# Squares, 1/rms and two staged reads in other places of a hybrid block's start-up order

## The chip, the core and the metric

The kernel runs on one core of a Trainium2 chip. Times are device microseconds (us) of one execution. TensorE is called PE here, VectorE DVE, ScalarE ACT, GpSimd POOL, and SyncE, which only sends DMAs here, SP. Times inside the execution count from the start of the profiled span.

## The reference

One layer: an RMSNorm of x (512 tokens, 2048 wide), one input projection whose columns are q, k, v, an attention gate, the input xr of a linear recurrence (LRU) and its gate, then attention beside the LRU, a norm and a gate on each, and an output projection added to x.

```python
def rms_norm(x, w):
    y = xf * lax.rsqrt(jnp.mean(xf * xf, axis=-1, keepdims=True) + EPS)
    return y * w
...
h = rms_norm(x, norm_w)
proj = jnp.einsum('bsd,de->bse', h, w_in)
q, k, v, g_attn, xr, g_lru = jnp.split(proj, SPLITS, axis=-1)
attn_out = attention_group(q, k, v, q_norm_w, k_norm_w)
lru_out = lru_group(xr, conv_w, conv_b, lru_wa, lru_ba, lru_wx, lru_bx, lru_lambda)
mixed = jnp.concatenate([rms_norm(attn_out, attn_norm_w) * jax.nn.silu(g_attn),
                         rms_norm(lru_out, lru_norm_w) * jax.nn.silu(g_lru)], axis=-1)
return x + jnp.einsum('bse,ed->bsd', mixed, w_out)
```

All in float32.

## The kernel before

**Products.** Every float32 operand is split into a high part and the rest, and a product is three matmuls (`mm3`, lines 153 to 155). A tile of x is `x` in the profile's rows, a tile of weights is read as `wr`, its high part cast on ACT to `wh` (line 228) and its rest made on DVE as `wl` (line 229).

**The norm.** The gain `norm_w` is multiplied into x's tiles. The factor 1/rms of a token isn't: the projection runs on the x without it, and the factor is multiplied in when a result leaves PSUM. It needs the squares of all of x, so it is known late: `xsquare` (line 276) sums the squares of a chunk on ACT (line 278; for the first two chunks on DVE), `xstats` adds the chunks' sums on DVE (line 402), takes the power -0.5 on POOL (`rsqrt_mean`, lines 374 and 375), and `rows` lays the result out on DVE (lines 386 to 389), spreads it over all partitions with one matmul by ones (line 396) and copies that to `rbc` (line 397).

**The start.** x comes in eight chunks of 256 columns (`L`, 512 KB each). The first two are turned by PE. Each of the others is turned in blocks on DVE (`B`, line 291), written aside to DRAM in four DMAs (`D`, line 306), read back in whole rows in one DMA (`R`, line 313), multiplied by the gain on ACT (line 361) and split on ACT and DVE (`V`, lines 367 and 368). The read waits until the write has landed. Beside this the chunk's weights are read (`W`, line 215) and split (`S`, lines 228 and 229), and its squares taken (`Q`). PE multiplies chunk after chunk for the first half of xr (`proj_feat`, accumulators `pj`), and after chunk 1 puts two chunks of the second half (accumulators `mm`) in between.

**What sets the order.** SP and POOL, and for the start ACT and DVE too, run in the order in which the program issues; each engine runs its own list in order, and a waiting instruction holds up all behind it. The table `moves` (lines 1245 to 1256) gives that order: a key `(c, e)` is the place behind PE's step e of chunk c, a letter an action and the digit its chunk (`Z` takes the next step of `xstats`: the first one the sum and the power, the second one the layout). After key `(6, 0)` ACT and DVE go back to the scheduler, which orders what follows by its own estimates.

**After the start.** Two steps of chunk 7 later PE runs the spreading matmul, finishes chunk 7, takes 36 matmuls of the second half, and then the first product of the LRU (`lru_pair`). Its input is the accumulator times `rbc` (`ev`, lines 1286 and 503), put through a convolution (one step on ACT, line 536, three on DVE, line 541), and split (lines 546 and 547, `k`). The LRU's own weights are read by SP (line 515).

Of the kernel before, what the change touches and what calls it, by code (L numbers as in the profile page):

```python
# [63 lines left out]
def hybrid_kernel(  # L64
# [814 lines left out]
    P1, Q6, Q5, Q7, P2, Q3, Q4 = 0, 5, 4, 3, 2, 6, 1  # L879
# [356 lines left out]
    def vectors(_):  # L1236
# [19 lines left out]
    }  # L1256

    def move(step):
# [244 lines left out]
```

## Time and profile before

| what | value |
|---|---|
| time, 3 runs | 630.44 us median (629.39 to 632.7) |
| the profiled execution's own time | 633.15 us |
| its span | 631.4 us |
| mean granted PE clock | 0.995 |
| DMA, mean over the span | 207 GB/s |

The span is what lies between the first and the last recorded instruction. A row of the timeline gives the start, the duration and the operation, `out<-in`, and in brackets how long the engine had been idle and what released it. A matmul's duration overlaps the next one's, so PE's pace is read from the distance of two starts.

### The profile page before, as it was taken

The page shows a single profiled execution, that of the slowest core. Times are in us where ns is not written, and L with a number is a line of the kernel's source. Part 1 is how long each engine was busy: PE and PEld are TensorE (multiplying, and loading weights), DVE is VectorE, ACT ScalarE, POOL GpSimd, SP SyncE. Part 2 cuts the span into 40 slices and gives each one's busy share as a digit, 9 for nine tenths or more (in the row PEclk, how much of TensorE's full clock was granted, in tenths as well). Part 3 has the DMA queues.
Part 4 walks back from the last instruction along what each step waited for, and adds up shares of the span by engine and source line. Part 5 has one row for each costly group of instructions (what it writes and reads, how often), then busy time and mean ns, then how long its engine had stood idle before and what let it go on. Part 6 is the DMA issues. An engine that isn't in the chain of part 4 may idle for free.

```text
span 631.4 us, 8289 instructions
## 1 busy us (share of the span) xinstructions
PE 622.8 (99%) x2732; PEld 511.8 (81%) x2732; DVE 495.5 (78%) x789; ACT 360.8 (57%) x648; POOL 106.0 (17%) x142
## 2 busy tenths in 40 slices
PE   9999899999999999999999999999999999999997
PEld 7877688888888888888888888888888888888886
DVE  6674877997979896787887788549989867787776
ACT  4478379988966741645575557339355544433441
POOL 3000211111103352512123222100210001010010
PEclk9999899999999999999999999999999999999999
DMA  8998857584976479589669647842995777797262
GB/s 280 315 306 295 241 108 187 152 191 132 224 237 209 125 162 273 134 191 271 189 188 269 198 136 200 250 117 67 241 282 178 229 238 234 283 335 243 71 200 100
DMA packets 76219, 130.76 MB, mean 207 GB/s; under 512 B 6953, under 2 KB 31121, under 8 KB 76177
## 3 DMA queue, kind: packets, MB, share of 16 engines
q1 hardware_dynamic: 68064, 112.75, 57.5%
q0 software_dynamic: 7936, 17.36, 14.2%
q8 instruction: 21, 0.34, 0.2%
q10 hardware_dynamic: 176, 0.14, 0.1%
q14 instruction: 22, 0.17, 0.1%
HBM read 111.87 MB, written 39.32 MB: 239 GB/s over the span
## 4 chain that ended last, share of the span: by engine, by line
PE 83%; DVE 7%; DMA 6%; ACT 2%; issue 1%; SPq 1%; POOL 0%; ACTq 0%; DVEq 0%
PE pj L154 16%; PE pj L155 15%; PE pj L153 15%; PE mm L1066 14%; PE pj L1066 11%; PE mm L154 4%; PE mm L153 4%; PE mm L155 4%; DMA wr<-in_w_in_dram 2%; DMA xu<-xd 2%; DVE wl L229 1%; DMA xd<-xu 1%; DVE k L541 1%; DVE xu L291 1%; DVE b L585 1%
## 5 line engine op out<-in xcount | busy, mean ns | idle before, releaser
L228 ACT CAST wh<-wr 128x512 fp32r<-128x512 f32 x142 | 84.3, 617 | 83.3 <-PE pj L154 33.1
L155 PE MATMUL pj<-x,wl 128*128 128x512 f32 x304 | 119.1, 392 | 0.2 <-DVE wl L229 0.2
L154 PE MATMUL pj<-x,wh 128*128 128x512 f32 x304 | 118.7, 391 | 0.0
L153 PE MATMUL pj<-x,wh 128*128 128x512 f32 x304 | 118.7, 390 | 0.0
L229 DVE TENSOR_TENSOR wl<-wr,wh 128x512 fp32r<-128x512 f32 x144 | 98.8, 713 | 23.8 <-ACT wh L228 21.3
L914 ACT CAST wh<-wr 128x1024 fp32r<-128x1024 f32 (+1 forms) x72 | 60.7, 860 | 75.7 <-PE mm L1066 37.2
L915 DVE TENSOR_TENSOR wl<-wr,wh 128x1024 fp32r<-128x1024 f32 (+1 forms) x72 | 68.7, 983 | 29.0 <-ACT wh L914 28.9
L153 PE MATMUL pj<-wh,x 128*128 128x512 f32 x192 | 74.9, 390 | 0.0
L154 PE MATMUL pj<-wl,x 128*128 128x512 f32 x192 | 74.8, 390 | 0.0
L155 PE MATMUL pj<-wh,x 128*128 128x512 f32 x192 | 74.7, 389 | 0.0
L155 PEld LDWEIGHTS pj<-x,wl 128*128 128x128 f32 x304 | 57.3, 188 | 13.3 <-DVE wl L229 1.3
L153 PEld LDWEIGHTS pj<-x,wh 128*128 128x128 f32 x304 | 57.2, 188 | 11.9 <-ACT wh L228 0.3
L154 PEld LDWEIGHTS pj<-x,wh 128*128 128x128 f32 x304 | 57.2, 188 | 11.9
L938 POOL DMA_DIRECT2D t<-in_w_out_dram x40 | 33.3, 890 | 141.8 <-DMA t<-in_w_out_dram 84.1
L1066 PE MATMUL mm<-wh,ml 128*128 128x512 f32 x126 | 49.0, 389 | 0.0
L1066 PE MATMUL mm<-wh,mh 128*128 128x512 f32 x126 | 49.0, 389 | 0.0
L1066 PE MATMUL mm<-wl,mh 128*128 128x512 f32 x126 | 49.0, 389 | 0.0
L153 PEld LDWEIGHTS pj<-wh,x 128*128 128x128 f32 x192 | 36.0, 188 | 8.1 <-ACT ev L628 0.5
L154 PEld LDWEIGHTS pj<-wl,x 128*128 128x128 f32 x192 | 36.1, 188 | 7.8 <-DVE wl L229 0.5
L155 PEld LDWEIGHTS pj<-wh,x 128*128 128x128 f32 x192 | 36.0, 188 | 7.5
L738 POOL TENSOR_SCALAR p<-p,sm 128x512 f32<-128x512 f32 x32 | 24.2, 759 | 89.6 <-DVE sm L737 89.6
L1066 PE MATMUL pj<-wl,mh 128*128 128x512 f32 (+1 forms) x100 | 38.5, 385 | 0.0
(229 smaller groups left out, 1176.2 us busy)
## 6 DMA issues: line engine op xcount, KB each, us to landing
wr<-in_w_in_dram SPq DMA_DIRECT2D x71, 512.0 KB, 5.0
wr<-in_w_out_dram SPq DMA_DIRECT2D x21, 512.0 KB, 5.6
t<-in_w_out_dram POOLq DMA_DIRECT2D x40, 256.0 KB, 7.6
wr<-t SPq DMA_DIRECT2D x40, 256.0 KB, 5.4
pd<-u SPq DMA_DIRECT2D x16, 512.0 KB, 3.0
pt<-pd SPq DMA_DIRECT2D x64, 128.0 KB, 3.7
t<-in_w_out_dram SPq DMA_DIRECT2D x24, 256.0 KB, 4.8
wr<-in_w_out_dram SPq DMA_DIRECT2D x22, 256.0 KB, 5.0
```

What stands on the lines that cost most here:

```text
L153: nc.tensor.matmul(acc, lh, rh, start=start, stop=False)
L154: nc.tensor.matmul(acc, lh, rl, start=False, stop=False)
L155: nc.tensor.matmul(acc, ll, rh, start=False, stop=stop)
L228: copy(hi, raw[:, k, :]).ins,
L229: nc.vector.tensor_sub(lo, raw[:, k, :], f(hi)).ins,
L291: nc.vector.transpose(u[:, :, :, t, :].rearrange("p b k r -> p k b r"), src.rearrange("p (k b c) -> p k b c", k=2, c=B),)
L541: nc.vector.scalar_tensor_tensor(xc[:, d0:d1], xr[:, d0 + o : d1 + o], v1(R_CW + j * NB + n), xc[:, d0:d1], op0=ALU.mult, op1=ALU.add,)
L738: last_pool[0] = nc.gpsimd.tensor_scalar(p, p, sm, 0.0, op0=ALU.mult, op1=ALU.add).ins
L914: nc.scalar.copy(hi[:, to], b)
L915: nc.vector.tensor_sub(lo[:, to], b, f(hi[:, to]))
L938: nc.gpsimd.dma_start(dst, src, accum_op=ALU.add)
L1066: nc.tensor.matmul(dst[s][:, es], lh[:, ts_], rh[:, es], start=i == ends_[0] and j == 0, stop=i == ends_[1] and j == 2,)
```

## The change

Only the table is edited. With letters as above:

```diff
-        (1, 0, 1): "V2 S2 W3 R4 L6 Q1 B5 D5",
-        (2, 0): "V3 S3 W4 L7 B6 D6 R5 W5",
-        (3, 0): "V4 Q2 S4 B7 D7 R6 W6",
-        (4, 0): "C2 V5 S5 Q5 W7 R7",
-        (5, 0): "C3 V6 S6 Q6",
-        (6, 0): "V7 S7 Q7 Q4 Z0 Z0 C3",
+        (1, 0, 1): "V2 S2 Q2 W3 R4 L6 Q1 B5 D5",
+        (2, 0): "V3 S3 W4 L7 B6 R5 D6 W5",
+        (3, 0): "V4 Q4 S4 Q5 B7 R6 D7 W6",
+        (4, 0): "C2 V5 S5 Q6 W7 R7",
+        (5, 0): "C3 V6 S6 Q7 Z0",
+        (6, 0): "V7 S7 Z0 C3",
```

Nothing is added or taken away: the rounds of squares of chunks 2, 4, 5, 6 and 7 stand in other places, the sum and power stand ahead of chunk 7's work, and the reads of chunks 5 and 6 stand ahead of the writes of chunks 6 and 7.

On ACT, from chunk 6's weights on, before (`wh_643` and `wh_647` are chunk 6's weights, `xu_526` is chunk 7's x read back, and the two rows `b_..,ssq` ahead of `wh_823` are the squares of chunks 7 and 4):

```order
L228 CAST wh_643<-wr_537 128x512
L228 CAST wh_647<-wr_537 128x512
L278 ACTIVATE b_69_402,ssq<-b_69_402 128x256 x4
L361 ACTIVATE xu_526<-xu_526,nw 128x4x128 x2
L367 CAST x_116_681<-xu_526 128x4x4x32
L367 CAST x_118_685<-xu_526 128x4x4x32
L228 CAST wh_689<-wr_600 128x512
L228 CAST wh_693<-wr_600 128x512
L278 ACTIVATE b_82_463,ssq<-b_82_463 128x256 x4
L278 ACTIVATE b_36_257,ssq<-b_36_257 128x256 x4
L228 CAST wh_823<-wr_821 128x512
```

and in the changed kernel (`wh_651` and `wh_655` are chunk 6's weights, `b_82_467` is chunk 7):

```order
L228 CAST wh_651<-wr_545 128x512
L228 CAST wh_655<-wr_545 128x512
L278 ACTIVATE b_82_467,ssq<-b_82_467 128x256 x4
L361 ACTIVATE xu_534<-xu_534,nw 128x4x128 x2
L367 CAST x_116_693<-xu_534 128x4x4x32
L367 CAST x_118_697<-xu_534 128x4x4x32
L228 CAST wh_701<-wr_608 128x512
L228 CAST wh_705<-wr_608 128x512
L228 CAST wh_823<-wr_821 128x512
```

Chunk 7's squares are now where chunk 6's were, and none stand behind chunk 7's weights.

On DVE at the same place, before (`xsum` is the sum, `x_117` and `x_119` are chunk 7's x, `wl_690` and `wl_694` its weights, `two` and `k_124` the layout, `lc` small constants of the LRU):

```order
L368 TENSOR_TENSOR x_117_682<-xu_526,x_116_681 128x4x4x32
L368 TENSOR_TENSOR x_119_686<-xu_526,x_118_685 128x4x4x32
L229 TENSOR_TENSOR wl_690<-wr_600,wh_689 128x512
L229 TENSOR_TENSOR wl_694<-wr_600,wh_693 128x512
L402 TENSOR_REDUCE xsum<-ssq 128x4
L386 CAST two<-rstd 64x4
```

and in the changed kernel, on to the copy of 1/rms (`rbc`); the layout's rows `two` and `k_124` read as before and are left out between the two pieces:

```order
L402 TENSOR_REDUCE xsum<-ssq 128x4
L368 TENSOR_TENSOR x_117_694<-xu_534,x_116_693 128x4x4x32
L368 TENSOR_TENSOR x_119_698<-xu_534,x_118_697 128x4x4x32
L229 TENSOR_TENSOR wl_702<-wr_608,wh_701 128x512
L229 TENSOR_TENSOR wl_706<-wr_608,wh_705 128x512
L386 CAST two<-rstd 64x4
```

```order
L229 TENSOR_TENSOR wl_828<-wr_821,wh_827 128x512
L482 TENSOR_TENSOR lc_575<-lc_575,lc_574 128x16
L483 TENSOR_SCALAR lc_575<-lc_575 128x16
L482 TENSOR_TENSOR lc_575<-lc_575,lc_574 128x16
L483 TENSOR_SCALAR lc_575<-lc_575 128x16
L484 TENSOR_TENSOR lc_575<-lc_575,lc_573 128x16
L486 TENSOR_SCALAR lc_571<-vec 128x16
L487 SCALAR_TENSOR_TENSOR lc_571<-lc_575,lc_571 128x16
L397 COPY rbc<-pj_766 128x512
```

The sum stands four instructions earlier, and seven small ones now stand between `wl_828` and `rbc`, where one stood before. Further on the scheduler also swapped a pair on ACT: the convolution's first step (line 536) stands ahead of the cast of `wh_914`, no longer behind it.

On SP, the writes and reads of chunks 5 to 7, before (`xd_471` and `xd_531` are the writes of chunks 6 and 7, `xu_409`, `xu_466`, `xu_526` the reads of chunks 5, 6 and 7, `wr` weights):

```order
L306 DMA xd_471<-xu_465 32x4x256 x4
L313 DMA xu_409<-xd_414 128x1024
L215 DMA wr_477<-in_w_in_dram 128x2x512
L306 DMA xd_531<-xu_525 32x4x256 x4
L313 DMA xu_466<-xd_471 128x1024
L215 DMA wr_537<-in_w_in_dram 128x2x512
L215 DMA wr_600<-in_w_in_dram 128x2x512
L313 DMA xu_526<-xd_531 128x1024
```

and in the changed kernel (`xd_476` and `xd_540` are the writes of chunks 6 and 7):

```order
L313 DMA xu_413<-xd_418 128x1024
L306 DMA xd_476<-xu_469 32x4x256 x4
L215 DMA wr_481<-in_w_in_dram 128x2x512
L313 DMA xu_470<-xd_476 128x1024
L306 DMA xd_540<-xu_533 32x4x256 x4
L215 DMA wr_545<-in_w_in_dram 128x2x512
L215 DMA wr_608<-in_w_in_dram 128x2x512
L313 DMA xu_534<-xd_540 128x1024
```

The reads of chunks 5 and 6 each stand ahead of the next chunk's write; the last read keeps its place.

## The prediction

> **What bounds the kernel now.** I read the page's engine totals first, then granted clock and busy time by stretch (windows), then PE's list of waits. Columns of the windows: stretch, length, busy time of PE, PEld, DVE, ACT and POOL, granted PE clock, DMA share, GB/s.
>
> ```profile
> PE 622.8 (99%) x2732; PEld 511.8 (81%) x2732; DVE 495.5 (78%) x789; ACT 360.8 (57%) x648; POOL 106.0 (17%) x142
> ...
> 62.00:66.00 4.00, 1.87 (x6) 1.44 (x6) 3.21 (x11) 1.06 (x3) 1.59 (x2) 0.86 1.02 283
> 66.00:82.00 16.00, 14.44 (x51) 11.07 (x50) 12.53 (x27) 8.46 (x14) 2.51 (x3) 0.82 0.86 214
> 82.00:140.00 58.00, 58.00 (x257) 48.01 (x256) 50.66 (x72) 50.59 (x76) 6.63 (x8) 1.00 0.64 156
> 36.00:52.00 16.00, 15.85 (x70) 12.63 (x69) 10.71 (x32) 11.04 (x31) 0.00 (x0) 1.00 1.00 332
> ...
> PE pj L396 <- DVE lc L482: 2.1, 1, 2.1
> PE pj L153 <- ACT k L546: 1.3, 1, 1.3
> ```
>
> PE is the bound, 99% busy, so only lost PE time can be won back. Between 62 and 82 it is idle twice, and just there the granted clock falls to 0.86 and 0.82; from 82 to 140 it is busy throughout at 1.00. The first wait is the matmul that spreads 1/rms, the second the LRU's first product. PE's timeline says what each costs:
>
> ```profile
> 46.87 0.50 PE L155 MATMUL pj<-x,wl 128*128 128x512 f32 x1 [0.15 <-DVE wl L229]
> ...
> 61.77 0.39 PE L155 MATMUL pj<-x,wl 128*128 128x512 f32 x1
> 64.29 0.47 PE L396 MATMUL pj<-k,ones_r 128*128 128x512 f32 x1 [2.13 <-DVE lc L482]
> ...
> 64.82 0.58 PE L154 MATMUL pj<-x,wh 128*128 128x512 f32 x1
> ...
> 68.46 0.40 PE L154 MATMUL mm<-x,wh 128*128 128x512 f32 x1
> ...
> 68.93 0.39 PE L153 MATMUL mm<-x,wh 128*128 128x512 f32 x1
> ...
> 75.50 0.39 PE L155 MATMUL mm<-x,wl 128*128 128x512 f32 x1
> 77.23 0.51 PE L153 MATMUL pj<-k,k 128*128 128x512 f32 x1 [1.34 <-ACT k L546]
> 77.96 0.50 PE L154 MATMUL pj<-k,k 128*128 128x512 f32 x1 [0.22 <-DVE k L547]
> ...
> 78.53 0.62 PE L153 MATMUL pj<-k,k 128*128 128x512 f32 x1
> ...
> 82.17 0.40 PE L153 MATMUL mm<-x,wh 128*128 128x512 f32 x1
> ```
>
> PE's pace is 0.227: 29 steps from 68.93 to 75.50. Against it four amounts are lost. **A**, the first wait: 2.52 from 61.77 to 64.29, less one step, 2.29. **B**, slow matmuls behind it: nine steps from 64.82 to 68.46 take 3.64 where 2.04 would do, 1.60. **C**, the second wait: four steps from 75.50 to 78.53 take 3.03 where 0.91 would do, 2.12. **D**, slow matmuls again: nine steps from 78.53 to 82.17, 3.64, 1.60 lost. Together 7.61 us, nearly all that the change can reach.
>
> [...]
>
> **The sum and the power of 1/rms.** What ends the first wait, on ACT, DVE and POOL:
>
> ```profile
> 53.60 0.19 ACT L278 ACTIVATION_READ_ACCUMULATOR b<-b 128x1 f32 x1
> 54.37 1.34 ACT L361 ACTIVATE xu<-xu,nw 128x512 f32<-128x512 f32 x2 [0.58 <-DMA xu<-xd]
> ...
> 57.69 0.41 ACT L278 ACTIVATE b<-b 128x256 f32<-128x256 f32 x1
> ...
> 60.81 0.19 ACT L278 ACTIVATION_READ_ACCUMULATOR b<-b 128x1 f32 x1
> 60.90 1.12 ACT L228 CAST wh<-wr 128x512 fp32r<-128x512 f32 x2
> ...
> 57.46 1.29 DVE L229 TENSOR_TENSOR wl<-wr,wh 128x512 fp32r<-128x512 f32 x2
> 61.03 0.19 DVE L402 TENSOR_REDUCE xsum<-ssq 128x4 f32<-128x32 f32 x1 [2.28 <-ACT b L278]
> 61.59 1.05 POOL L375 TENSOR_TENSOR rstd<-rstd,nhalf 128x4 f32<-128x4 f32 x1
> 62.68 0.16 DVE L386 CAST two<-rstd 64x4 fp32r<-64x4 f32 x1 [1.46 <-POOL rstd L375]
> ...
> 63.45 0.69 DVE L389 TENSOR_TENSOR k<-both,two 128x512 fp32r<-128x512 f32 x1
> 64.06 0.17 DVE L482 TENSOR_TENSOR lc<-lc,lc 128x16 f32<-128x16 f32 x1
> ```
>
> Two rounds of squares (57.69 to 61.00) stand between chunk 7's weights and the sum. In the changed kernel chunk 7's round takes the place that chunk 6's has now, whose last row ends at 53.79; chunks 4 and 2 have moved into earlier gaps of ACT. The sum then runs at about 53.9 and the power, 1.6 later (61.03 to 62.64 now), ends at about 55.5, beside chunk 7's work. The layout stands behind `wl`, which ends at 58.75; it takes 1.46 (62.68 to 64.14), so it is done at 60.2. PE reaches the spreading matmul at 61.77 + 0.23 = 62.0. **A is won whole, 2.29**, with 1.8 us to spare, and B with it: 1.60.
>
> The new wait is the sum's on DVE: behind it stand chunk 7's two subtractions, and PE waits for those. They can't start before chunk 7's x lands (54.37 on ACT) and is multiplied, so the sum, waiting until 53.9, costs nothing; it would if the round ended later than about 56. The squares moved forward are five rounds of some 1.6 us, the same number as before, each in a place where ACT waits for a DMA or DVE or where a round stood already: nothing.
>
> **The second wait.** After A and B, PE runs the 43 matmuls from the spreading one through the row now at 75.50 from 62.0 to 62.0 + 43 x 0.227 = 71.8. What has to be there is `k`:
>
> ```profile
> 65.51 0.68 DVE L397 COPY rbc<-pj 128x512 f32<-128x512 f32 x1
> ...
> 72.30 0.62 ACT L228 CAST wh<-wr 128x512 fp32r<-128x512 f32 x1 [4.44 <-PE mm L154]
> 72.83 0.81 ACT L536 ACTIVATE k<-ev,vec 128x512 f32<-128x512 f32 x1
> ...
> 74.94 1.53 DVE L541 SCALAR_TENSOR_TENSOR k<-ev,vec,k 128x511 f32<-128x511 f32 x2
> ...
> 76.56 0.62 ACT L546 CAST k<-k 128x512 fp32r<-128x512 f32 x1 [2.41 <-DVE k L541]
> ```
>
> The copy to `rbc` can begin when the spreading matmul is out, 62.5, and when DVE is through with two `wl` (1.25 after 60.2) and seven small constants, about 0.2 each: 62.9, against 65.51. Behind it come two constants and six operations of 0.61 (as 63.45 to 64.06 above: one evacuation, two `wl`, one split, two evacuations), to 67.3; the convolution on ACT, 0.8, which no longer stands behind a cast that waits for PE (4.44 now); on DVE two steps (1.53), two `wl`, a third step, 3.5 in all, to 71.6; and the cast of `k`, to 72.2. PE is there at 71.8: it waits about 0.4, then about 0.6 more until DVE has the rest of `k` (0.73 from 77.23 to 77.96 now), and a little at each start. I take 1.2 for what is left of C, between none and the 2.12 of now: **0.9 won**. Whether 1.2 us of waiting still halves the clock no row shows: 2.12 did, and the small one at 46.87 did not (36 to 52: clock 1.00). Nearer the lower one, and spread over two pieces, I take D as won, 1.60, with a rival for the other end.
>
> **The reads ahead of the writes.** SP's rows now, then how long the pieces of all writes (line 306) take to land, then all such reads (line 313), of which the last one, sent at 46.30, has the 8.0:
>
> ```profile
> 36.59 1.88 SPq L306 DMA_DIRECT2D xd<-xu  x4
> 38.57 0.41 SPq L313 DMA_DIRECT2D xu<-xd  x1
> ...
> 42.20 1.77 SPq L306 DMA_DIRECT2D xd<-xu  x4
> 44.07 0.40 SPq L313 DMA_DIRECT2D xu<-xd  x1
> ...
> DMA to landing us min/median/max: 2.6/3.8/5.9
> ...
> DMA to landing us min/median/max: 4.1/4.6/8.0
> ```
>
> Chunk 5's read goes out up to 1.9 earlier, but waits for chunk 5's write; behind it now queue chunk 6's write, 0.5 later (39.0 at its end), then chunk 6's read, which waits for that write (39.0 + 3.8 = 42.8), and behind it chunk 7's write, 43.2 to 45.0, one us later than now. Two weight reads (1.2) stand ahead of the last read, which waits for 45.0 + 3.8 = 48.8: 2.5 later than its 46.30. Its 8.0 to landing is 3.4 over the 4.6 that such reads take as a median, since two weight reads are ahead of it in the DMA engines; an issue 2.5 later takes from that surplus first. So chunk 7's x lands where it does, at 54.4, and so do its weights' products: **nothing**, between 0.9 won (an issue as now) and the loss in the rival.
>
> **Sum:** 2.29 + 1.60 + 0.9 + 1.60 = 6.4. The profiled execution took 633.15; it would take 626.75. The median of the runs is 2.71 lower; I carry that over: 630.44 - 6.4 = **624.0**.
>
> **The rivals.**
> 1. The rest of the second wait still halves the clock: D stays, the gain is 4.8, 625.6. For it: 2.12 did, and no row shows from what length on. Chance 0.24.
> 2. The lead is lost on DVE and ACT. From 82 to 140 they are busy 50.66 and 50.59 of 58 us, so neither can catch up by more than 7 us; if ACT's order holds them to the lead that `rbc` has, 65.5 - 62.9 = 2.6, PE waits for them later: 627.8. Against: ACT's 4.44 and 2.41 of waiting in the rows above fall away, more than the 3.8 missing. Chance 0.15.
> 3. SP's new waits delay chunk 7 and the kernel is slower. With both writes at the slowest landing, 5.9, chunk 6's read goes at 44.9, chunk 7's write ends at 47.1, the last read goes at 53.0 and, with 8.0, lands at 61.0: 6.7 later. PE idles for it and runs slow behind it (1.6): 8.3 against 6.4 won, 632.3. It is slower from 4.8 of delay on. Against: the surplus above. Chance 0.05, some of it with an even longer landing.
> 4. The slow steps don't come from the waits and stay without them: only A and 0.9 of C are won, 3.2, and it comes to 627.2. [...] Against: both slow stretches begin right behind the two waits, and from 82 to 140, without a wait, the clock is 1.00. Chance 0.06.
> 5. The sum isn't what holds the spreading matmul, and nothing changes: 630.4. Against: DVE's layout ends at 64.14, PE starts at 64.29. Chance 0.05.
>
> **How the numbers follow.** The forecast has 0.45. Its own bounds: no second wait left gives 1.2 more, 622.8; the range begins at 622.4 with a little from chunks 5 and 6 and ends at 628.6, past rivals 1, 4 and 2; outside lie 3 and 5 and ends of the forecast. About 0.5%, 3.15 us, is what a measurement of this kernel can tell from no change, so faster means under 627.3: the forecast, rival 1, and parts of 2 and 4, 0.75. Within 0.5%: the rest of 2 and 4, rival 5 and most of 3, 0.21. Slower: 0.04.
>
> **What would show it.** The sum right behind chunk 7's squares at about 54 and the power done before chunk 7's weights are split; the spreading matmul without a wait of its own and steps of 0.227 behind it (A, B); the LRU's first product near 72, with about 1 us of waiting, then no steps near 0.40 (C, D); chunk 7's x on ACT near 54.4 (the reads); PE without new waits between 82 and 150 (rival 2). I am wrong if the last read lands after 56, if the LRU's weights come later than `rbc`, or if the granted clock still falls below 1.00 after 62.

## The result and the profile after

| | before | changed kernel |
|---|---|---|
| time, 8 runs each | 630.71 us median (629.39 to 632.7) | 627.24 us median (626.45 to 629.21) |
| the profiled execution's own time | 633.15 us | 626.45 us |
| its span | 631.4 us | 624.4 us |
| its mean granted PE clock | 0.995 | 1.0 |

The ratio is 0.9945, 95% interval 0.9928 to 0.9963: 3.5 us faster. The forecast was 624.0 in a range of 622.4 to 628.6, so the sign and the range held, and the number was 3.2 us too low. The two profiled executions, though, lie 6.70 us apart, which is close to the forecast sum of 6.4. Both are true, and the experiments are about the difference. (Two executions of the experiments, of 777.61 and 1217.89 us at clocks of 0.754 and 0.908, lie far from all others of the same kernels and are left out everywhere.)

The windows of the changed kernel, with the columns as before:

```profile
62.00:66.00 4.00, 4.00 (x20) 3.28 (x19) 3.90 (x13) 1.76 (x3) 0.00 (x0) 1.00 1.00 266
66.00:82.00 16.00, 15.56 (x68) 12.34 (x67) 13.67 (x20) 10.72 (x17) 3.44 (x4) 1.00 1.00 226
82.00:140.00 58.00, 58.00 (x258) 48.04 (x257) 52.76 (x75) 50.45 (x76) 6.64 (x8) 1.00 0.67 167
```

The clock is 1.00 in all three, where it was 0.86 and 0.82 in the first two, and from 62 to 66 PE has no gap. Its timeline there:

```profile
61.85 0.39 PE L155 MATMUL pj<-x,wl 128*128 128x512 f32 x1
62.07 0.40 PE L396 MATMUL pj<-k,ones_r 128*128 128x512 f32 x1
62.31 0.39 PE L153 MATMUL pj<-x,wh 128*128 128x512 f32 x1
...
71.61 0.39 PE L155 MATMUL mm<-x,wl 128*128 128x512 f32 x1
72.22 0.51 PE L153 MATMUL pj<-k,k 128*128 128x512 f32 x1 [0.22 <-ACT k L546]
72.94 0.50 PE L154 MATMUL pj<-k,k 128*128 128x512 f32 x1 [0.22 <-DVE k L547]
73.27 0.39 PE L155 MATMUL pj<-k,k 128*128 128x512 f32 x1
73.51 0.40 PE L153 MATMUL pj<-k,k 128*128 128x512 f32 x1
```

The spreading matmul (L396) starts one step behind its neighbour and waits for nothing: A is gone. No step behind it is slow: B is gone. Of C four steps from 71.61 to 73.51 are left, 1.90 where 0.91 would do: 0.99 lost instead of 2.12. No slow steps follow: D is gone too. The LRU's first product starts at 72.22 instead of 77.23. The matmul that ends D before (row 82.17) starts at 75.57, 6.60 earlier, and the last matmul of all 6.96 earlier (620.49, not 627.45), so nearly all of the difference between the two traces arises here.

The work that releases PE, on ACT, DVE and POOL:

```profile
53.84 0.19 ACT L278 ACTIVATION_READ_ACCUMULATOR b<-b 128x1 f32 x1
54.48 1.34 ACT L361 ACTIVATE xu<-xu,nw 128x512 f32<-128x512 f32 x2 [0.44 <-DMA xu<-xd]
...
71.54 0.62 ACT L546 CAST k<-k 128x512 fp32r<-128x512 f32 x1 [1.77 <-DVE k L541]
...
54.07 0.18 DVE L402 TENSOR_REDUCE xsum<-ssq 128x4 f32<-128x32 f32 x1 [0.84 <-ACT b L278]
...
59.53 0.69 DVE L389 TENSOR_TENSOR k<-both,two 128x512 fp32r<-128x512 f32 x1
...
62.73 0.69 DVE L397 COPY rbc<-pj 128x512 f32<-128x512 f32 x1
...
54.63 1.05 POOL L375 TENSOR_TENSOR rstd<-rstd,nhalf 128x4 f32<-128x4 f32 x1
```

The sum (L402) is at 54.07 behind chunk 7's squares, the power (L375) ends at 55.68 beside chunk 7's work, and the layout ends at 60.22, 1.85 ahead of PE. On SP the last two reads (L313):

```profile
43.36 0.34 SPq L313 DMA_DIRECT2D xu<-xd  x1
43.81 1.89 SPq L306 DMA_DIRECT2D xd<-xu  x4
45.73 1.28 SPq L215 DMA_DIRECT2D wr<-in_w_in_dram  x2
49.98 0.34 SPq L313 DMA_DIRECT2D xu<-xd  x1
```

The last one goes out 3.7 later than before (46.30), and chunk 7's x is on ACT at 54.48 against 54.37: the later issue costs next to nothing.

### The profile page after: what moved, and what is told of

The parts are those of the page before. It is cut to its first block, busy times and chain, and to the rows that moved or that the text cites. A ratio compares the mean times of both kernels' runs of the same rounds, so it can differ in the third digit from the quotient of the medians.

```text
span 624.4 us, 8293 instructions
## 1 busy us (share of the span) xinstructions
PE 618.8 (99%) x2732; PEld 508.8 (81%) x2732; DVE 495.7 (79%) x789; ACT 361.1 (58%) x648; POOL 105.6 (17%) x142
## 4 chain that ended last, share of the span: by engine, by line
PE 91%; DMA 5%; DVE 2%; ACT 1%; SPq 1%; issue 0%; ACTq 0%; DVEq 0%
PE pj L154 18%; PE pj L155 17%; PE pj L153 17%; PE mm L1066 14%; PE pj L1066 11%; PE mm L155 5%; PE mm L153 5%; PE mm L154 5%; DMA wr<-in_w_in_dram 3%; DMA xu<-xd 1%; DVE xu L291 1%; DMA xd<-xu 1%; DVE wl L229 1%; ACT xu L361 0%; ACT wh L228 0%
## 5 line engine op out<-in xcount | busy, mean ns | idle before, releaser
L938 POOL DMA_DIRECT2D t<-in_w_out_dram x40 | 33.3, 893 | 142.5 <-DMA t<-in_w_out_dram 81.8
```

Source lines behind the costliest of these rows:

```text
L938: nc.gpsimd.dma_start(dst, src, accum_op=ALU.add)
```

## The experiments

**Theory:** the squares and the sum carry all of the gain through A and C, the two waits are in every execution of the kernel before, and the slow steps behind them (B, D) only in some of them. Each execution lists its mean granted clock, and a stretch of slow steps lowers it by about 0.0027 (in the trace of before the clock is 0.50 from 78.53 to 81.94, 3.41 us of the 631.4), so by this theory the clock counts the stretches. **Rivals:** the reads carry part of the gain; the slow steps belong to every execution and the change pays for them elsewhere.

**1. The kernel before once more**, beside a second set of itself.

> The kernel before, unchanged. Theory (clock): the slow matmuls behind PE's two waits come in some executions and not in others, and the profiled execution of before (633.15 us, mean granted clock 0.995) had both, the most there can be; each slow stretch is 1.6 us and 0.0027 of mean clock. Then the executions show mean clocks of 0.995, 0.997 and 1.000, and their times fall with the clock: about 632.5, 631 and 629.3. Rival (run to run): all executions have the same slow stretches, clock 0.995 in each, and their times of 629.4 to 632.7 differ through something outside 62 to 82 us. Either way ratio 1.000.

631.62 us against 631.34, ratio 0.9994 (0.9981 to 1.0006). Put together with the runs of the kernel before that went along with the later experiments, on four chips, this gives 99 executions:

| mean granted clock | executions of before | median us |
|---|---|---|
| 0.999 or 1.0 | 46 | 630.23 |
| 0.997 | 47 | 631.92 |
| 0.994 to 0.996 | 5 | 633.39 |

(One more, at 0.947, took 631.34 and fits no row.) The time rises by 1.69 and by 1.47 from row to row, close to the 1.60 of B and of D, so each row is read as one stretch of slow steps more. The traces agree: two stretches at 0.995 (the first trace, and experiment 3), one at 0.997 (experiment 12), none at 1.0 in the changed kernel. Whether the waits are shorter in the fast rows, too, isn't shown, since only two of these executions (the first trace and experiment 12) are read step by step. By this reading a little under half of the executions have no stretch, half have one, and 1 in 20 has both. The profile that I forecast from, 633.15 at 0.995, is one of those. The changed kernel, 14 executions with those of experiment 9, is at 0.999 or 1.0 in all of them, with a median of 627.33.

**2. The squares and the sum alone**, the reads back behind the writes:

```diff
 (of the changed kernel)
-        (2, 0): "V3 S3 W4 L7 B6 R5 D6 W5",
-        (3, 0): "V4 Q4 S4 Q5 B7 R6 D7 W6",
+        (2, 0): "V3 S3 W4 L7 B6 D6 R5 W5",
+        (3, 0): "V4 Q4 S4 Q5 B7 D7 R6 W6",
```

> The changed kernel with the reads of chunks 5 and 6 put back behind the writes of chunks 6 and 7. Theory (squares): all of the gain is that the spreading matmul (line 396) no longer waits for 1/rms; this kernel gains what the change gained, ratio 0.9945 within 0.0015, spreading matmul without a wait near 62.0, LRU's first product near 72.2. Rival (reads): the reads carry a part, and the ratio is above 0.997.

627.44 us, ratio 0.9934 (0.9915 to 0.9953), all clocks at 0.999 or 1.0. The whole gain is there without the reads.

**3. The reads alone:**

```diff
 (of the kernel before)
-        (2, 0): "V3 S3 W4 L7 B6 D6 R5 W5",
-        (3, 0): "V4 Q2 S4 B7 D7 R6 W6",
+        (2, 0): "V3 S3 W4 L7 B6 R5 D6 W5",
+        (3, 0): "V4 Q2 S4 B7 R6 D7 W6",
```

> The kernel before with only the two reads put ahead of the next chunk's write. Theory (squares): ratio 1.000 within 0.0015; the spreading matmul still waits 2.1 us, chunk 7's x still reaches ACT at 54.4 within 0.5. Rival (reads): ratio below 0.998. Second rival (queue): SP's new waits bring chunk 7's x after 55.4 and the ratio is above 1.001.

633.29 us, ratio 1.0029 (1.0013 to 1.0045): alone they are a small loss, though the theory had none and chunk 7's x is on ACT at 54.72, in time. PE's waits and the windows:

```profile
PE pj L396 <- DVE lc L482: 2.1, 1, 2.1
PE pj L153 <- ACT k L546: 1.3, 1, 1.3
...
62.00:66.00 4.00, 1.88 (x8) 1.26 (x7) 2.87 (x11) 1.22 (x3) 1.93 (x2) 0.92 0.88 255
66.00:82.00 16.00, 14.43 (x51) 11.04 (x50) 12.52 (x27) 8.38 (x14) 2.51 (x3) 0.82 0.94 226
```

Both waits are as long as before, and the clock falls behind both. What differs, for the most part, is how often: 6 of 11 executions have both stretches (0.994 to 0.996), against none of the 33 of the kernel before on the same chip that fit the table. Why they have them more often wasn't found.

**4. The rest of C.** `C3`, the last of the LRU's small constants, ahead of chunk 7's work, and the accumulator's first product with `rbc` (L1286) ahead of the other work:

```diff
 (of the changed kernel)
-        (5, 0): "C3 V6 S6 Q7 Z0",
-        (6, 0): "V7 S7 Z0 C3",
+        (5, 0): "C3 V6 S6 Q7 Z0 C3",
+        (6, 0): "V7 S7 Z0",
...
-            with tc.high_priority():
+            with tc.high_priority(AHEAD):
                 next(stats)
                 nc.vector.tensor_mul(done[0], done[0], rbc)
```

> The changed kernel, with the last small constants of the LRU moved ahead of chunk 7's work, and the accumulator that the LRU needs first multiplied by rbc right behind the copy to rbc. Theory: the convolution's input is there some 3 us earlier, the LRU's first product finds its input and PE's rest of the second wait (0.97 us in the changed kernel) goes to 0; the rest of the program moves up by 0.6 to 1.0 us, ratio to the kernel before 0.993 (about 626.4). Rival: DVE and ACT, busy 91% and 87% from 82 to 140, take it back at the wait near 141 (0.3 us in the changed kernel), which grows by as much; ratio 0.9945.

627.26 us, ratio 0.993 (0.9907 to 0.9952): as far from before as the squares alone on the same chip. PE's timeline and DVE's part of the windows (the third busy time):

```profile
50.89 0.39 PE L155 MATMUL pj<-x,wl 128*128 128x512 f32 x1
52.88 0.50 PE L153 MATMUL pj<-x,wh 128*128 128x512 f32 x1 [1.60 <-ACT wh L228]
...
141.44 0.50 PE L154 MATMUL pj<-wl,x 128*128 128x512 f32 x1 [0.42 <-DVE wl L229]
...
147.44 0.50 PE L154 MATMUL pj<-wl,x 128*128 128x512 f32 x1 [0.23 <-DVE wl L229]
...
66.00:82.00 16.00, 16.00 (x72) 13.23 (x72) 14.24 (x21) 10.41 (x17) 3.46 (x4) 1.00 0.94 222
...
100.00:141.00 41.00, 41.00 (x181) 33.62 (x180) 40.93 (x57) 32.36 (x52) 5.02 (x6) 1.00 0.62 151
```

PE has no gap from 66 to 82, so the rest of C was won. But DVE is busy 40.93 of the 41 us from 100 to 141 (in the changed kernel 40.93 too, where PE is busy 41.00 and doesn't wait for it), and PE, now earlier, waits for DVE at 141 and 147. The wait at 52.88 is for a weight read that landed late (ACT stood 2.80 for it).

**5. The sum behind chunk 7's work**, the squares still early:

```diff
 (of the changed kernel)
-        (5, 0): "C3 V6 S6 Q7 Z0",
-        (6, 0): "V7 S7 Z0 C3",
+        (5, 0): "C3 V6 S6 Q7",
+        (6, 0): "V7 S7 Z0 Z0 C3",
```

> The changed kernel with the sum and the power put back behind chunk 7's weights; the squares stay moved. Theory (round): the rounds of squares behind chunk 7 made the wait, the sum's own place does not matter: the sum starts near 58.8, the layout is done near 62.0, just when PE comes to the spreading matmul; its wait is under 0.3 us and the ratio is that of the changed kernel, 0.994. Rival (sum): the sum's place made a large part of it, the wait is over 1 us and the ratio above 0.997.

629.34 us, ratio 0.9976 (0.9958 to 0.9994): missed. I had taken the place of the sum to matter little once the squares are early. PE and DVE:

```profile
74.18 0.50 PE L153 MATMUL pj<-k,k 128*128 128x512 f32 x1 [1.57 <-ACT k L546]
...
59.36 0.17 DVE L402 TENSOR_REDUCE xsum<-ssq 128x4 f32<-128x32 f32 x1
...
60.99 0.16 DVE L386 CAST two<-rstd 64x4 fp32r<-64x4 f32 x1 [1.46 <-POOL rstd L375]
...
64.45 0.68 DVE L397 COPY rbc<-pj 128x512 f32<-128x512 f32 x1
```

The spreading matmul (62.66 in this trace) still doesn't wait, so A is won by the squares alone. But DVE now stands 1.46 behind the sum, waiting for the power, ahead of the layout, and all that follows there is late: `rbc` begins 1.79 behind the spreading matmul's start, where it was 0.66 (62.07 to 62.73), and the LRU's first product waits 1.57. So by the medians more than half of the gain hangs on the sum's place, by way of C; a part of this is that 3 of the 10 executions are at 0.997.

**6. One round of squares back behind chunk 7's weights:**

```diff
 (of the changed kernel)
-        (5, 0): "C3 V6 S6 Q7 Z0",
-        (6, 0): "V7 S7 Z0 C3",
+        (5, 0): "C3 V6 S6",
+        (6, 0): "V7 S7 Q7 Z0 Z0 C3",
```

> The changed kernel with chunk 7's round of squares, the sum and the power behind chunk 7's weights: one round there, where the kernel before has two. Theory (round): the spreading matmul waits 0.6 to 0.8 us, 1.6 less than before; too short for the slow clock, so every execution has a mean clock of 0.999 or 1.000, and the ratio is about 0.995. Rival (clock by any wait): executions at 0.997 appear.

628.86 us, ratio 0.997 (0.9952 to 0.9988), a little more than the theory's 0.995. The spreading matmul waits 0.57 in the trace, and all 10 executions are at 0.999 or 1.0: with waits like this and the 1.17 and 0.22 that the trace has at C, none shows slow steps.

**7. Three rounds behind them**, in the kernel before (two there):

```diff
 (of the kernel before)
-        (4, 0): "C2 V5 S5 Q5 W7 R7",
+        (4, 0): "C2 V5 S5 W7 R7",
...
-        (6, 0): "V7 S7 Q7 Q4 Z0 Z0 C3",
+        (6, 0): "V7 S7 Q7 Q4 Q5 Z0 Z0 C3",
```

> The kernel before with a third round of squares (chunk 5's) behind chunk 7's weights, nothing else: the suspected wait lengthened. Theory (clock by the wait, hit or missed by where it falls): the spreading matmul waits 3.7 to 3.9 us, a slow stretch of about 1.6 us follows it in nearly every execution (mean clock 0.997 or below in at least 9 of 10, against half of the executions of before), and the ratio is 1.003 to 1.004. Rival (clock not by this wait): the share of executions at 0.997 stays near half, and the ratio is 1.0025, the 1.6 us alone.

635.87 us, ratio 1.0077 (1.0049 to 1.0104), more than the theory's 1.003 to 1.004. PE, DVE and POOL say why:

```profile
70.20 0.77 PE L396 MATMUL pj<-k,ones_r 128*128 128x512 f32 x1 [6.17 <-DVE lc L482]
70.76 0.63 PE L153 MATMUL pj<-x,wh 128*128 128x512 f32 x1
...
64.00 0.19 DVE L402 TENSOR_REDUCE xsum<-ssq 128x4 f32<-128x32 f32 x1 [3.87 <-ACT b L278]
...
65.36 0.91 POOL L938 DMA_DIRECT2D t<-in_w_out_dram  x1 [51.65 <-DMA t<-in_w_out_dram]
66.34 0.19 POOL L374 TENSOR_SCALAR rstd<-xsum 128x4 f32<-128x4 f32 x1
66.60 0.88 POOL L938 DMA_DIRECT2D t<-in_w_out_dram  x1
67.18 1.37 POOL L375 TENSOR_TENSOR rstd<-rstd,nhalf 128x4 f32<-128x4 f32 x1
```

The sum comes 2.97 later than before (61.03): 1.6 by the round and 1.4 because ACT comes to chunk 7's x later (55.76, not 54.37). On POOL the power then falls in among the issues of the output weights' reads (L938): POOL stands until 65.36 for the first of them, which is ahead of the power's first instruction (L374), and sends another between the power's two. It ends at 68.55, 4.36 behind the sum's end, instead of 1.42. So the price of a late round isn't linear. The clock part held: all 6 executions are at 0.994 or 0.995, so none escaped. In the trace the granted clock is already 0.69 from 64.00 to 70.00, while PE is busy for 0.03 of the 6.00 us, and 0.61 from 70.00 to 74.00, so here the mean clock counts more than the slow steps behind the wait.

**8. The constants of q and k early**, to take work from DVE's full stretch: 4 with the reads as in 2, and the norm weights of q and k read ahead into a buffer of their own.

```diff
 (of the kernel of 4, with the reads as in 2)
-            wb = k2(shape=(P, 2, HD))
-            nc.sync.dma_start(wb[:, 0, :], src[None, :].broadcast_to([P, HD]))
+            wb = pools["rope"].tile([P, 2, HD], F32, name=nm("wb"), tag="wb", bufs=2)
+            with tc.issue_after(last_x):
+                nc.sync.dma_start(wb[:, 0, :], src[None, :].broadcast_to([P, HD]))
```

> The kernel mul_first with the reads of chunks 5 and 6 back behind the writes, and the gains of the q and k norms loaded early into tiles of their own, so that DVE does not wait for them near 97 us. Theory (DVE takes it back): mul_first had no second wait but lost 0.8 and 0.7 us of PE time near 141 and 147, where DVE, 2.4 us of which went to waiting for these loads, was late; this kernel has those waits under 0.4 us together and gains 0.8 to 1.5 us on squares_only, ratio 0.9915. Rival: DVE is late there for its work, not for the loads; ratio 0.993 to 0.9935, as mul_first and squares_only.

630.83 us, ratio 1.0007 (0.9987 to 1.0028): theory and rival both missed. DVE and PE:

```profile
81.56 0.23 DVE L614 TENSOR_SCALAR wb<-wb 128x128 f32<-128x128 f32 x1 [5.96 <-DMA wb<-in_q_norm_w_dram]
...
105.74 0.50 PE L153 MATMUL pj<-k,k 128*128 128x512 f32 x1 [1.21 <-ACT b L558]
...
107.87 0.80 PE L153 MATMUL pj<-k,k 128*128 128x512 f32 x1 [1.17 <-ACT b L558]
108.47 0.63 PE L154 MATMUL pj<-k,k 128*128 128x512 f32 x1
```

The second constant's read went out only at 72.6, behind other work of SP, and landed late. DVE stood 5.96 us for it, and PE 0.99 at 82.70; ACT's order changed too, and PE waited twice near 106, with slow steps behind that (0.43 from 108.47 to 111.03). The profiled execution (632.72 us at 0.997) is one of the slower ones, but the seven of 12 at 0.999 or 1.0 have a median of 629.89, as the kernel before has in such executions on this chip (629.91): the gain is gone in them too. So this kernel doesn't tell whether DVE is late at 141 for its work or for these loads.

**9 to 11. The changed kernel, the kernel of 2, and 4 without the reads**, side by side on one chip. (What the last expectation calls weights of the first LRU pair are the small constants `C3`.)

> The changed kernel as it is, beside the kernel before and the two others on one chip. By the theory (PE's lost time A and about half of C are gone for certain, the slow steps B and D only in the executions that had them) its ratio to before lies at 0.9930 to 0.9950, and the mean granted clock of no execution is under 0.998. By the rival (the gain of 3.5 us was a matter of the chip it was measured on) the ratio lies outside 0.992 to 0.997.

> The changed kernel with the reads of chunks 5 and 6 behind the writes again, as before. By the theory that the reads ahead of the writes cost nothing of their own once the spreading matmul no longer waits, it comes within 0.1% (0.6 us) of the changed kernel, on either side. By the rival that they cost what they cost alone (0.29%), it is 1.2 to 1.8 us faster than the changed kernel.

> The squares and the sum moved, the reads as before, and the weights of the first LRU pair and its products taken from chunk 6 on: the early move of C3 and the higher priority, without the reads. By the theory that the rest of C can be won if nothing is taken back between 50 and 53 us (that wait was for a weight read, which the order of the reads moved), it is 0.8 to 1.5 us faster than the changed kernel. By the rival (DVE is busy without a gap from 100 to 141, so what PE gains at 72 it loses at 141 to 147 again) it is within 0.6 us of it.

| kernel | us | ratio to before (630.64) |
|---|---|---|
| changed | 627.69 | 0.994 (0.9916 to 0.9964) |
| squares and sum only | 627.72 | 0.9944 (0.9922 to 0.9967) |
| the same, and the edit of 4 | 627.17 | 0.995 (0.9931 to 0.9969) |

The gain repeats on another chip, and beside the squares the reads cost and bring nothing that the runs can tell (0.03 us). Most of what the edit of 4 wins is taken back, even without the late weight read: PE waits for DVE at 141 and 147 for 0.9, where the kernel of 2 waits 0.36 at 142. In the traces of experiments 10 and 11 PE is 1.13 ahead of the kernel of 2 at the 340th matmul behind the spreading one (139.77 against 140.90), and 0.25 at the 400th (154.95 against 155.20). The medians differ by 0.55, inside the rival's 0.6, and two of the 12 executions with the edit of 4 are at 0.996 and 0.997. No version beats the change by more than the runs can tell.

**12. A second trace of before.**

> The kernel before, unchanged, for a second trace of it. By the theory (the two waits A and C are in every execution, the slow steps behind them only in some) its profiled execution shows the spreading matmul waiting 1.9 to 2.3 us and the LRU's first product 1.2 to 1.5 us, and, with a chance of 9 in 10, at most one of the two stretches of slow steps, at a mean clock of 0.997 or more. By the rival (waits and slow steps come and go together) a clock of 0.997 or more goes with one of the two waits being under 1 us.

631.2 us; the profiled execution took 633.29 at a clock of 0.997. PE's timeline:

```profile
65.15 0.47 PE L396 MATMUL pj<-k,ones_r 128*128 128x512 f32 x1 [1.60 <-DVE lc L482]
65.45 0.40 PE L153 MATMUL pj<-x,wh 128*128 128x512 f32 x1
65.69 0.39 PE L154 MATMUL pj<-x,wh 128*128 128x512 f32 x1
...
77.32 0.50 PE L153 MATMUL pj<-k,k 128*128 128x512 f32 x1 [2.16 <-ACT k L546]
...
78.62 0.50 PE L153 MATMUL pj<-k,k 128*128 128x512 f32 x1
78.92 0.63 PE L154 MATMUL pj<-k,k 128*128 128x512 f32 x1
79.34 0.63 PE L155 MATMUL pj<-k,k 128*128 128x512 f32 x1
...
81.90 0.52 PE L155 MATMUL pj<-k,k 128*128 128x512 f32 x1
82.26 0.40 PE L153 MATMUL mm<-x,wh 128*128 128x512 f32 x1
```

Both waits are there and one stretch of slow steps, D without B, as the theory has it; the lengths it gave were off both ways (1.60 and 2.16, for 1.9 to 2.3 and 1.2 to 1.5). The LRU's first product still starts at 77.32, where it was 77.23 with B: PE was through with the work ahead of it earlier, and waited longer.

## Why the prediction was right, and where its size failed

**A:** right. The sum was forecast at about 53.9, the power's end at 55.5, the layout's end at 60.2 and the spreading matmul at 62.0; they are at 54.07, 55.68, 60.22 and 62.07. Experiments 5 and 6 show that A hangs on the squares: with the sum late A stays gone, with one round late 0.57 of waiting comes back.

**C:** right. `rbc` at 62.9 (62.73), the cast of `k` done at 72.2 (72.16), PE there at 71.8; 1.2 left to lose, 0.99 measured. Experiment 5 shows that this part comes from the sum's place.

**The reads:** right, nothing. The last read was forecast at 48.8 and went at 49.98, chunk 7's x was forecast at 54.4 and came at 54.48. Experiments 2, 9 and 10 agree; alone (3) they lose 0.29%.

**B and D: the sum took them as costs of every execution, 1.60 each, and this is the step that failed.** The waits do cause them: they are in executions with the waits, in all six with the longest wait, in none of the 14 of the changed kernel, and in none of the 12 of experiments 2 and 10. (Experiment 11 has two executions with a lower clock, whose waits no trace shows.) So rival 4, whose 627.2 happens to be the time measured, is wrong in its mechanism. But in half of before's executions one is there, and both in 1 of 20. The profiled execution had both, and its 2.71 over the median was mostly this: 633.15 is 2.92 above the 630.23 of the executions without a stretch, near twice 1.60. I carried the 2.71 over as an offset that has nothing to do with the change, and took off B and D besides. Counted from executions without a stretch, A and the part of C, forecast at 2.29 + 0.9 = 3.2, are 630.23 - 627.33 = 2.9, over all chips; on the one chip of experiment 9 it is 629.95 - 627.69 = 2.3. The rest of the gain is what the stretches add to the median of before, 630.92 - 630.23 = 0.7 of the forecast 3.2.

Nor are the terms independent: in the second trace of before B is gone and C is longer by 0.82, since the first product waits for `k`, not for PE. From the spreading matmul to that product it is 12.94 with B (64.29 to 77.23) and 12.17 without (65.15 to 77.32). So in this pair B's 1.60 cost 0.77 by then, and the rest lay hidden behind the wait for `k`. That is an estimate from two traces, of which the second also had chunk 7's x on ACT 0.9 later.

**Rival 1** (the rest of C still halves the clock) is wrong: 14 executions at 0.999 or 1.0. **Rival 2** was wrong for the change (PE 58.00 of 58 from 82 to 140), yet its limit is there and decides experiments 4 and 11: behind DVE's full stretch up to 141 most of what PE gains beyond this change is lost again (1.13 ahead, then 0.25). **Rivals 3 and 5** didn't occur.

Left open: at a clock of 1.0 the changed kernel's executions still differ by up to 2.8 us (626.45 to 629.21). Its trace in experiment 9 (628.17 us) has the LRU's first product at 73.87 instead of 72.22, behind waits for chunks and weights between 40 and 55; why their reads land later in some executions wasn't tried.

## What to carry to other kernels

Before terms of one trace are subtracted from a median, ask whether the profiled execution is a typical one: its time and clock beside those of many executions say whether a cost in it is paid always or sometimes, and the offset between trace and median may be that very cost. A gain on the engine that bounds the kernel can end at the next engine without slack: here the first 3 us were kept, and most of what came on top was taken back 70 us later. Put the early links of a chain (a sum, a power) where nothing else waits, and look at the chain's end, not only at the first wait that it releases.

## What the runs showed of the hardware

**Slow steps behind short waits, but not always.** In the kernel before a wait of 2.13 had nine steps of 0.40 on average behind it, so had waits of 1.34 and 0.22 close together, while 1.60 had none in the second trace (row 65.15; the granted clock from 62 to 66 was 1.00), nor in experiment 4 (row 52.88; 1.00 from 48 to 62), and in experiment 5, with 1.57 and 0.22, 3 of 10 executions were at 0.997. In the first trace the granted clock was 0.51 from 64.82 to 68.28 and 0.50 from 78.53 to 81.94, with steps of 0.43 within both, and 1.00 from 68.30 to 77.20, with steps of 0.23 up to 75.50. The slow steps end at about 68.28 (the step from 68.19 takes 0.27, mostly at full pace) and 81.94, which is 13.66 apart. In the second trace the steps from 78.62 and 81.90 take 0.30 and 0.36, between the paces of 0.23 and 0.43, so the slow steps run from about 78.77 to 82.18, an estimate of 3.41, as long as from 78.53 to 81.94 in the first. How much idling it takes isn't settled. In the first trace the waits of 1.34 and 0.22, 1.56 together, had slow steps behind them; the 1.60 of the second trace (63.55 to 65.15) had none. Nor do the traces tell whether the place of the wait or its length decides from one execution to the next: A had slow steps behind it at 2.13, and at 2.12 in experiment 3, and none at 1.60.

**A power on POOL ended 1.42 us behind its sum with POOL free and 4.36 us behind it with two DMA issues around it** on POOL's queue, for the first of which POOL had to wait (experiment 7).
